# Attention's half of the output projection as 32 column-half units, half of them placed between later heads

## The chip, the cores and the metric

One core of one Trainium2 chip runs one layer of a hybrid encoder in one launch. The metric is the device time of the launch in microseconds (us); lower is better. The engines have short names in the views: PE is TensorE's matmuls, PEld its weight loads, DVE is VectorE, ACT is ScalarE, POOL is GpSimd, and SP is SyncE, which issues every transfer of this kernel. An engine works through its own queue in order; a semaphore wait stops everything behind it on that engine.

## The reference

The sequence has 2048 rows of 1024 features. After a normalisation one projection feeds two groups of heads, and one output projection takes both:

```
h    = rms_norm(x, norm_w);  proj = h @ w_in
dn   = gated_deltanet_bidir(q, k, v, beta, decay)      # 4 heads of 128, chunks, forward and backward
dn   = rms_norm(dn) * silu(z)
sw   = windowed_gqa_with_sinks(q, k, v) * silu(z)       # 8 query heads, |i-j| <= 128
out  = x + concat([dn, sw]) @ w_out                     # w_out: 1024 x 1024
```

Rows 512 to 1023 of `w_out` belong to attention (`sw`). Their product needs nothing of the delta rule, so it can be computed, added to `x` and stored as a partial result at any time between the end of attention and the last stage.

## The kernel before

Matmuls that need precision without full fp32 cost are split: an operand is copied to the fp32r type by ACT (the high part), DVE subtracts to get the low part, and three fp32r matmuls (high times high, low times high, high times low) replace one.

**phase_a** projects, convolves, runs attention (chunks of 128 rows, two groups of heads each, `attend` L327 to L378) and writes the gated attention result of each chunk to DRAM (`mix_sw`, L378).

**phase_b** has these parts, in program order:

- `pre_front(h)` (L604) loads keys, queries and values of head h, transposes them, forms the gram products `gh` (L661), multiplies them by the decay on DVE (`ma`, L670) and stores the result to DRAM (`m_d`, L675).
- `out_sw` (L564) is attention's half of the output. `load_wo` (L534) splits all of attention's rows of `w_out` (two tiles of 16 KB per partition). For each of 16 chunks it loads the mix tile once (L569), splits it (L550 on ACT, L551 on DVE), and for each of two column halves of 512 loads the rows of `x` (L555), runs 12 matmuls (L558 to L560), adds on DVE (L561) and stores a partial result (L562). Mix and split tiles have two buffers, the tag `ws` (weights in flight and `x` rows) five.
- `pre_back(h)` (L689) inverts the triangular matrices: it loads diagonal blocks (L697, L698), runs a chain of 31 pairs of dependent DVE instructions (L707, L711: the solve), stores and reloads the result (L712, L720), and assembles the inverse from 20 groups of matmuls `pi` (L735) with POOL copies between them.
- `scan(h)` (L761) is the recurrence: 16 steps, forward and backward side by side, each with five small fp32 matmuls (`pk`, `py`, `po`) joined by DVE and ACT instructions. `post` (L818) normalises and stores.
- `warm(h)` (L847) issues 32, 32 and 20 matmuls with an unused result, at the end of heads 1, 2 and 3.
- `out_dn` (L873) does the other half of the output, from the delta rule's result plus the stored partials.

`out_sw` lives in a memory pool `sw` on the right side of SBUF; the pool `hd[1]`, which holds the matrices, keys and values of heads 1 and 3, is opened after it is closed, in the same place. So nothing of head 1 can be written into `hd[1]` before the last of the 16 chunks is done.

The order on each engine isn't the program's. `set_order` (L892) lists all instructions with estimated costs, plans forwards and backwards several times with those costs, and fixes the best plan as the order of every queue. A gate in it stands for each reuse of a buffer and for each pool that takes the place of a closed one. The queue orders named below are read from the two compiled programs.

Of the kernel before, what the change touches and what calls it, by code (L numbers as in the profile page):

```python
# [7 lines left out]
F32 = mybir.dt.float32  # L8
F32R = mybir.dt.float32r
AF = mybir.ActivationFunctionType  # L10
ALU = mybir.AluOpType
# [4 lines left out]
P = 128  # L16
# [3 lines left out]
NCH = 16  # L20
# [3 lines left out]
EPS = 1e-6  # L24
NDEC = 1
NEG = -1e30


# [488 lines left out]
def phase_b(ctx, tc, t, ident, consts, hp, mix_dn, mix_sw, kq_d, v_d, zdn_d, zsw_d, dp, out):  # L517
    nc = tc.nc
    V, A, G, T = nc.vector, nc.scalar, nc.gpsimd, nc.tensor
    dma = nc.sync.dma_start  # L520

    def pool(name, bufs=1, stack=ctx, **kw):
        return stack.enter_context(tc.tile_pool(name=name, bufs=bufs, reuse_waits="tile", **kw))
# [8 lines left out]
    part_d = [dp.tile([P, D], F32, tag=f"part{c}", name=f"part{c}") for c in range(NCH)]  # L532
# [30 lines left out]

    def out_sw(pool, bank, order):  # L564
        w = load_wo(pool, 4, "s", "s")
        for n, c in enumerate(order):
            sc = slice(c * P, (c + 1) * P)
            mx = pool.tile([P, 4, P], F32, tag="mx", name=f"mxs{c}", bufs=2)
            dma(mx, mix_sw[c])  # L569
            out_half(pool, lambda j, nm: bank(n, j, nm), w, mx, t["x"][sc, :], part_d[c], f"s{c}", MB)  # L570

    MB = 2
    ORD = (7, 8, 6, 9, 5, 10, 4, 11, 3, 12, 2, 13, 1, 14, 0, 15)
    pre_stack = ctx.enter_context(ExitStack())
    with tc.using_default_side("right"):
        hd = [pool("hd0"), None]
        q1 = pool("q1")
        ps_i = [pool("ps_i0", stack=pre_stack, space=PSUM)]
        ps_t = pool("ps_t", stack=pre_stack, space=PSUM)
        ps_g = pool("ps_g", stack=pre_stack, space=PSUM)  # L580
    rp = pool("rp", 2)
    qp = pool("qp", stack=pre_stack)
    ps_s = pool("ps_s", space=PSUM)
# [20 lines left out]
    def pre_front(h):  # L604
# [12 lines left out]
        for n, c4 in enumerate(FRONT):  # L617
# [71 lines left out]
    def pre_back(h, H):  # L689
        ma = H["ma"]  # L690
        m_d, x_d, mp = H["solve"]
        L0 = qp.tile([64, 32, 32], F32, tag="L0", name=f"L0{h}")
# [7 lines left out]
        G.memset(x, 0.0)  # L700
# [146 lines left out]
    def warm(h):  # L847
        idle = ps_s.tile([P, P], F32, tag="pk", name=f"warm{h}")
        for _ in range((32, 32, 20)[h]):
            T.matmul(idle, ident, ident, start=True, stop=True)  # L850

    H = pre_front(0)
    with tc.using_default_side("right"):
        with ExitStack() as sw:
            out_sw(
                pool("sw", 5, stack=sw),
                lambda n, j, nm: ps_i[j if n >= 6 else 0].tile([P, 512], F32, tag="inv", name=nm),
                range(NCH),
            )
# [28 lines left out]

SBUF_BYTES = 229344 - 16512


def set_order(tc):  # L892
# [12 lines left out]
    def aps(l):  # L905
        return [a.bass_ap for a in l if hasattr(a, "bass_ap")]
# [142 lines left out]

# [5 lines left out]
    for k in range(total):  # L1055
        if eng[k] == "SP":
# [180 lines left out]
```

## Time and profile before

| | us |
|---|---|
| three runs | 1333.45, 1336.02, 1339.87 (median 1336.02) |
| span of the profiled execution | 1337.1 |
| PE busy | 1265.9 |
| DVE busy | 886.6 |
| ACT busy | 707.6 |
| POOL busy | 487.9 |

The launch has seven stages. Up to about 735 us it is projections, convolutions and attention. From 735 to 840 attention's last chunks run beside the front of head 0 and the first units of `out_sw`. From 840 to 896 the rest of `out_sw` runs beside the solve of head 0. Then come the four heads, bounded by the first inverse product of each: 896, 1002, 1098 and 1172 us. In each head's stage its scan runs together with the front and the solve of the next head. From 1242 us on the delta rule's half of the output runs to the end.

A matmul's busy time in these views covers its way through the array, so neighbours overlap: a busy PE isn't a PE at its peak. Where a view gives a count and a time for matmuls one after another, the time divided by the count is the better price.

### The profile page before, as it was taken

What the parts mean: (1) busy time and instruction counts of PE and PEld (TensorE: products, weight loads), DVE (VectorE), ACT (ScalarE), POOL (GpSimd) and SP (SyncE); (2) the same over time, 40 slices, a digit from 0 to 9 for tenths busy, and PEclk for the clock granted to TensorE, in tenths of its full rate; (3) what the DMA queues carried; (4) which work ended last, traced back from release to release, by engine and by line L of the source; (5) the groups of instructions that cost most, each with busy time, mean ns of one, the idle gap of its engine ahead of it and who ended that gap; (6) DMA issues with size and microseconds to landing.
All of it is one profiled execution on the core that took longest, in us unless ns stands there. A gap on an engine that the chain in (4) does not pass through costs nothing.

```text
span 1337.1 us, 22922 instructions
## 1 busy us (share of the span) xinstructions
PE 1265.9 (95%) x7330; PEld 1083.1 (81%) x7330; DVE 886.6 (66%) x2250; ACT 707.6 (53%) x2105; POOL 487.9 (36%) x876
## 2 busy tenths in 40 slices
PE   5999999999999999999999899999979989898998
PEld 4998878888789988888888678778869878798776
DVE  4413387999856324778987898567884987846433
ACT  5422254766544333334766866229757867566310
POOL 1223033575602321002677654328238247070000
PEclk8999999999999999999999999999999999999999
DMA  7442344222552444323222767968476364333776
GB/s 243 129 139 82 115 142 133 98 88 93 177 178 88 134 146 135 114 71 105 87 94 93 264 198 228 279 197 214 121 193 171 97 198 117 97 107 107 230 239 216
DMA packets 219113, 199.10 MB, mean 149 GB/s; under 512 B 48240, under 2 KB 170736, under 8 KB 218992
## 3 DMA queue, kind: packets, MB, share of 16 engines
q1 hardware_dynamic: 218992, 197.63, 48.5%
q8 instruction: 59, 0.97, 0.3%
q14 instruction: 62, 0.51, 0.1%
HBM read 132.50 MB, written 65.08 MB: 148 GB/s over the span
## 4 chain that ended last, share of the span: by engine, by line
PE 67%; DVE 10%; DMA 9%; ACT 6%; POOL 3%; issue 2%; SPq 1%; DVEq 0%; POOLq 0%; ACTq 0%
PE pf_c L186 6%; PE pf_c L187 6%; PE pf_c L188 5%; PE pf_z L186 4%; PE pf_z L187 4%; PE pf_z L188 4%; PE pi L735 3%; PE pt L360 3%; PE pq_q L197 2%; PE pq_q L198 2%; PE pq_q L199 2%; PE pcd L559 2%; PE pcd L560 2%; PE pcd L558 2%; DMA xc<-x_d 2%
## 5 line engine op out<-in xcount | busy, mean ns | idle before, releaser
L237 DVE SCALAR_TENSOR_TENSOR acc<-pf_c,cw,acc 128x512 f32<-128x512 f32 (+1 forms) x192 | 140.1, 743 | 30.4 <-ACT acc L233 27.0
L186 PE MATMUL pf_c<-xhi,wh_c 128*128 128x512 f32 x384 | 148.7, 399 | 1.7 <-DVE acc L237 1.6
L187 PE MATMUL pf_c<-xlo,wh_c 128*128 128x512 f32 x384 | 148.5, 399 | 0.0
L188 PE MATMUL pf_c<-xhi,wl_c 128*128 128x512 f32 x384 | 147.7, 397 | 0.0
L355 POOL TENSOR_SCALAR pr<-pr,st 128x384 f32<-128x384 f32 (+1 forms) x128 | 84.4, 678 | 83.5 <-DVE st L353 59.1
L188 PE MATMUL pf_z<-xhi,wl_z 128*128 128x512 f32 x256 | 94.3, 400 | 0.0
L186 PE MATMUL pf_z<-xhi,wh_z 128*128 128x512 f32 x256 | 94.1, 399 | 0.0
L187 PE MATMUL pf_z<-xlo,wh_z 128*128 128x512 f32 x256 | 93.6, 397 | 0.0
L346 ACT ACTIVATE pr<-pr,st 128x384 f32<-128x384 f32 (+1 forms) x128 | 76.0, 596 | 27.1 <-DVE st L345 24.2
L186 PEld LDWEIGHTS pf_c<-xhi,wh_c 128*128 128x128 f32 x384 | 72.1, 188 | 17.6 <-DVE acc L237 2.2
L188 PEld LDWEIGHTS pf_c<-xhi,wl_c 128*128 128x128 f32 x384 | 72.1, 188 | 15.2
L187 PEld LDWEIGHTS pf_c<-xlo,wh_c 128*128 128x128 f32 x384 | 72.1, 188 | 14.3
L364 ACT ACTIVATE ph<-pt 128x512 fp32r<-128x512 f32 x92 | 53.7, 595 | 50.1 <-PE pt L360 42.4
L341 DVE CUSTOM_DVE_ANT_0 pr<-s,mask,sink 128x384 f32<-128x384 f32 (+1 forms) x128 | 72.9, 591 | 8.4 <-PE s L340 5.7
L360 PE MATMUL pt<-ident,pr 128*128 128x128 f32 x368 | 70.8, 276 | 2.5 <-POOL pr L355 2.1
L365 DVE TENSOR_TENSOR pl<-pt,ph 128x512 fp32r<-128x512 f32 x92 | 62.0, 683 | 12.7 <-ACT ph L364 11.6
L789 ACT ACTIVATE yk<-py,ck 128x128 f32<-128x128 f32 x120 | 44.1, 367 | 43.6 <-PE py L784 40.9
L360 PEld LDWEIGHTS pt<-ident,pr 128*128 128x128 f32 x368 | 47.8, 141 | 19.0 <-POOL pr L355 5.9
L670 DVE SCALAR_TENSOR_TENSOR ma<-gh,bp,dc 128x256 f32<-128x256 f32 x128 | 56.0, 475 | 10.2 <-PE gh L661 8.1
L233 ACT ACTIVATE acc<-pf_c,cw 128x512 f32<-128x512 f32 x48 | 32.6, 682 | 54.3 <-PE pf_c L188 48.8
L197 PE MATMUL pq_q<-wh_q,xhi 128*128 128x256 f32 x256 | 58.5, 284 | 0.2 <-ACT sgq L256 0.2
L561 DVE TENSOR_TENSOR xrd<-xrd,pcd 128x512 f32<-128x512 f32 x32 | 20.9, 683 | 55.8 <-PE pcd L560 48.0
(254 smaller groups left out, 3795.2 us busy)
## 6 DMA issues: line engine op xcount, KB each, us to landing
kqc<-kq_d SPq DMA_DIRECT2D x120, 128.0 KB, 2.6
ws_c<-wt SPq DMA_DIRECT2D x48, 256.0 KB, 3.6
xr<-x SPq DMA_DIRECT2D x16, 512.0 KB, 5.7
ws_z<-wt SPq DMA_DIRECT2D x32, 256.0 KB, 3.5
kq<-kq_d SPq DMA_DIRECT2D x16, 512.0 KB, 4.9
xrs<-x SPq DMA_DIRECT2D x32, 256.0 KB, 3.9
part<-xrs SPq DMA_DIRECT2D x32, 256.0 KB, 3.4
m_d<-ma SPq DMA_DIRECT2D x32, 256.0 KB, 4.8
```

Source lines behind the costliest of these rows:

```text
L186: T.matmul(ps, hi[:, k, cs], xhi[b][:, k], start=(k == 0), stop=False)
L187: T.matmul(ps, hi[:, k, cs], xlo[b][:, k], start=False, stop=False)
L188: T.matmul(ps, lo[:, k, cs], xhi[b][:, k], start=False, stop=(k == KC - 1))
L197: T.matmul(ps[:, :n], xh, hi[:, k, :n], start=(k == 0), stop=False)
L237: V.scalar_tensor_tensor(av, ps[:, lo:], cw[:, i, k : k + 1], av, ALU.mult, ALU.add)
L341: V.tensor_tensor_reduce(pr[j][:, :n], ps[:, :n], mask[:, lo * P : hi * P], 1.0, sink[:, hh : hh + 1], ALU.add, ALU.max, accum_out=mx[:, j ...
L346: A.activation(pr[j][:, :n], pr[j][:, :n], AF.Exp, bias=nm[:, j : j + 1], accum_out=den[:, j : j + 1])
L355: G.tensor_scalar(pr[j][:, :n], pr[j][:, :n], den[:, j : j + 1], 1.0, ALU.mult, ALU.mult)
L360: T.transpose(pt[:, j], pr[j][:, (kb - lo) * P : (kb - lo + 1) * P], ident)
L364: A.activation(ph, ptf, AF.Copy)
L365: V.tensor_tensor(pl, ptf, ph.bitcast(F32), ALU.subtract)
L670: V.scalar_tensor_tensor(ma[d, c4][:, c], gh[:, k], bp[:, d, cc : cc + 1], gms[d][:, c : c + 1].to_broadcast([P, 2, P]), ALU.mult, ALU.mult,)
```

## The change

Attention's half of the output becomes 32 units, one for each chunk and column half. All 16 units of column half 0 are written between `pre_front(0)` and `pre_back(0)` in the program; of column half 1, four are written into `pre_front(2)`, four into `pre_front(3)` and eight after `pre_back(3)`; the planner is free to move them. A unit loads and splits the whole mix tile for itself, so each mix tile is loaded and split twice. Mix and split tiles have one buffer each, `ws` two; the weights are held one column half at a time.

The pool `hd1` is opened on the left, in a place of its own. Room for it comes from the smaller buffers, from a smaller reserve for software-generated transfers (`SCRATCH`, 1024 bytes), and from dropping the tile `L0`: the solve's first blocks are now loaded into `X`, copied from there into `L`, and `X` is cleared afterwards. The unused matmuls of `warm` become none. Four costs of the planner are changed. The part of the diff that matters:

```diff
+SCRATCH = 1024
+N0 = 16
+FILLF = ((0, 0, 0, 0), (1, 1, 1, 1), (1, 1, 1, 1))
+SWB = (1, 1)
+SWW = 2
...
+    def sw_units(pool):
+        w = {}
+        def weights(j):
+            wh = pool.tile([P, 4, 512], F32R, tag="wohs", name=f"wohs{j}", bufs=1)
+            wl = pool.tile([P, 4, 512], F32R, tag="wols", name=f"wols{j}", bufs=1)
...
+        def unit(c, j, bank):
+            if j not in w:
+                weights(j)
+            wh, wl = w[j]
+            ns = slice(j * 512, (j + 1) * 512)
+            mx = pool.tile([P, 4, P], F32, tag="mx", name=f"mxs{c}_{j}", bufs=SWB[0])
             dma(mx, mix_sw[c])
+            mh = pool.tile([P, 4, P], F32R, tag="mh", name=f"mhs{c}_{j}", bufs=SWB[1])
+            ml = pool.tile([P, 4, P], F32R, tag="ml", name=f"mls{c}_{j}", bufs=SWB[1])
+            A.activation(mh, mx, AF.Copy)
+            V.tensor_tensor(ml, mx, mh.bitcast(F32), ALU.subtract)
+            xr = pool.tile([P, 512], F32, tag="ws", name=f"xrs{c}_{j}")
+            dma(xr, t["x"][c * P : (c + 1) * P, ns])
...
+        todo = [(c, j) for j in range(2) for c in range(NCH)]
...
-        hd = [pool("hd0"), None]
-        q1 = pool("q1")
+        hd = [pool("hd0")]
+        q1 = pool("q1", stack=pre_stack)
+        qp = pool("qp", stack=pre_stack)
...
+    hd.append(pool("hd1"))
     rp = pool("rp", 2)
-    qp = pool("qp", stack=pre_stack)
+    swp = pool("swp", SWW, stack=pre_stack)
...
+            if h:
+                for k in range(FILLF[h - 1][n]):
+                    fill(1, bank(k % 2))
...
-        dma(L0, lv[0])
+        dma(X[0:64], lv[0])
         dma(L[64:128], lv[1])
         x = X.rearrange("p r c -> p (r c)")
+        V.tensor_copy(L[0:64], X[0:64].rearrange("p r c -> p c r"))
         G.memset(x, 0.0)
         G.memset(x[:, ::33], 1.0)
-        V.tensor_copy(L[0:64], L0.rearrange("p r c -> p c r"))
...
-        for _ in range((32, 32, 20)[h]):
+        for _ in range((0,0,0)[h]):
...
     H = pre_front(0)
-            out_sw(
...
-        hd[1] = pool("hd1")
+    for n in range(N0):
+        fill(1, bank(2 + n % 2 if n >= 6 else 2))
     pre_back(0, H)
     for h in range(3):
         scan(h, H)
         H = pre_front(h + 1)
         pre_back(h + 1, H)
         warm(h)
+    for k in range(32):
+        fill(1, bank(k % 2))
     pre_stack.close()
...
-SBUF_BYTES = 229344 - 16512
+SBUF_BYTES = 229344 - SCRATCH - 128
...
-                return max(112, m / 2.4 + 14)
+                return max(112, 0.441 * m + 4)
...
-            return 60 + 0.86 * m + 85 * (scalars > 0) + 110 * (len(o) > 1)
+            short = len(o[0].ap) > 2 and o[0].ap[-1][1] <= 64
+            return 60 + 0.86 * m + 85 * (scalars > 0) + 110 * (len(o) > 1) + 100 * short
...
-        return 150 + 1.02 * m
+        return 190 + 1.02 * m
...
+        if eng[k] == "PE" and not insts[k][0].is_transpose and "float32r" not in str(insts[k][0].ins[0].dtype):
+            lag += 40
```

More of the change, by code (lines that the diff above doesn't have):

```diff
@@ L562, in out_half, with take @@
             dma(dst[:, ns], xr)
[L564 to L568, printed above, removed]
-            dma(mx, mix_sw[c])
-            out_half(pool, lambda j, nm: bank(n, j, nm), w, mx, t["x"][sc, :], part_d[c], f"s{c}", MB)
+    def sw_units(pool):
[3 more added lines that the diff above has]
+            wl = pool.tile([P, 4, 512], F32R, tag="wols", name=f"wols{j}", bufs=1)
+            for k in range(4):
+                st = pool.tile([P, 512], F32, tag="ws", name=f"woss{j}_{k}")
+                dma(st, t["wout"][:, 4 + k, j * 512 : (j + 1) * 512])
+                A.activation(wh[:, k], st, AF.Copy)
+                V.tensor_tensor(wl[:, k], st, wh[:, k].bitcast(F32), ALU.subtract)
+            w[j] = wh, wl
+        def unit(c, j, bank):
[4 more added lines that the diff above has]
+            mx = pool.tile([P, 4, P], F32, tag="mx", name=f"mxs{c}_{j}", bufs=SWB[0])
+            dma(mx, mix_sw[c])
+            mh = pool.tile([P, 4, P], F32R, tag="mh", name=f"mhs{c}_{j}", bufs=SWB[1])
[4 more added lines that the diff above has]
+            dma(xr, t["x"][c * P : (c + 1) * P, ns])
+            ps = bank(f"pcs{c}_{j}")
+            for k in range(4):
+                T.matmul(ps, mh[:, k], wh[:, k], start=(k == 0), stop=False)
+                T.matmul(ps, ml[:, k], wh[:, k], start=False, stop=False)
+                T.matmul(ps, mh[:, k], wl[:, k], start=False, stop=(k == 3))
+            V.tensor_tensor(xr, xr, ps, ALU.add)
+            dma(part_d[c][:, ns], xr)
+        todo = [(c, j) for j in range(2) for c in range(NCH)]
+        def take(n, bank):
+            for _ in range(min(n, len(todo))):
+                unit(*todo.pop(0), bank)
+        return take
     MB = 2
@@ L691, in pre_back @@
         m_d, x_d, mp = H["solve"]
-        L0 = qp.tile([64, 32, 32], F32, tag="L0", name=f"L0{h}")
         L = qp.tile([P, 32, 32], F32, tag="L", name=f"L{h}")
@@ L848, in warm, with bank @@
         idle = ps_s.tile([P, P], F32, tag="pk", name=f"warm{h}")
-        for _ in range((32, 32, 20)[h]):
+        for _ in range((0,0,0)[h]):
             T.matmul(idle, ident, ident, start=True, stop=True)
+    fill = sw_units(swp)
+    def bank(k):
+        return lambda nm: (ps_t, ps_g, ps_i[0], ps_i[1])[k].tile([P, 512], F32, tag=("tr", "gh", "inv", "inv")[k], name=nm)
     H = pre_front(0)
-    with tc.using_default_side("right"):
-        with ExitStack() as sw:
-            out_sw(
[L856 to L859, printed above, removed]
-        hd[1] = pool("hd1")
+    for n in range(N0):
+        fill(1, bank(2 + n % 2 if n >= 6 else 2))
     pre_back(0, H)
@@ L1227 @@
     arrays = layout(inputs)
-    nc = bacc.Bacc("TRN2", target_bir_lowering=False, num_devices=1)
+    nc = bacc.Bacc("TRN2", target_bir_lowering=False, num_devices=1, dynamic_dma_scratch_size=SCRATCH)
     t = {k: nc.dram_tensor(k, v.shape, mybir.dt.from_np(v.dtype), kind="ExternalInput").ap() for k, v in arrays.items()}
```

## Prediction, made before the changed kernel ran

> **What bounds the kernel now.** I read the page first: share of time by engine, slices, chain.
>
> ```profile
> span 1337.1 us, 22922 instructions
> PE 1265.9 (95%) x7330; PEld 1083.1 (81%) x7330; DVE 886.6 (66%) x2250; ACT 707.6 (53%) x2105; POOL 487.9 (36%) x876
> ...
> PE 67%; DVE 10%; DMA 9%; ACT 6%; POOL 3%; issue 2%; SPq 1%; DVEq 0%; POOLq 0%; ACTq 0%
> ```
>
> PE carries two thirds of the chain, but its 95% is an average over unlike stages. So next comes the view of stretches, cut where the first inverse product of each head starts (columns: length; busy time and count of PE, PEld, DVE, ACT, POOL; clock; transfers).
>
> ```profile
> 50.00:735.00 685.00, 679.82 (x3667) 576.23 (x3667) 454.59 (x978) 334.62 (x745) 245.00 (x377) 1.00 0.36 114
> 735.00:840.00 105.00, 99.18 (x512) 78.32 (x511) 90.37 (x277) 78.57 (x251) 54.46 (x70) 0.98 0.72 230
> 840.00:896.00 56.00, 50.96 (x217) 40.67 (x215) 38.11 (x91) 9.01 (x21) 12.01 (x20) 0.97 0.83 259
> 896.00:1002.00 106.00, 91.39 (x652) 81.75 (x652) 81.67 (x263) 78.44 (x350) 51.80 (x111) 0.98 0.65 169
> 1002.00:1098.00 96.00, 86.80 (x647) 79.82 (x648) 72.66 (x239) 72.18 (x302) 48.62 (x97) 0.97 0.59 162
> 1098.00:1172.00 74.00, 67.83 (x517) 62.42 (x518) 56.00 (x189) 44.82 (x167) 33.96 (x90) 0.98 0.39 106
> 1172.00:1242.00 70.00, 64.39 (x514) 60.52 (x512) 38.87 (x122) 48.46 (x176) 26.44 (x77) 1.00 0.39 116
> 1242.00:1337.00 95.00, 90.26 (x396) 72.23 (x395) 33.87 (x59) 15.79 (x42) 1.64 (x1) 0.99 0.67 225
> ```
>
> Up to 735 us and from 1242 us PE is the bound, and the work there is unchanged. ACT falls from 78.57 of 105 us to 9.01 of 56 at 840 us: attention is over. What then fills 840 to 896? The same view for attention's output units alone, then the chain in order of time:
>
> ```profile
> 735.00:840.00 105.00, 49.89 (x176) 31.73 (x177) 9.51 (x14) 0.98 0.72 230
> 840.00:896.00 56.00, 50.09 (x209) 39.68 (x207) 12.32 (x18) 0.97 0.83 259
> ```
>
> ```profile
> 840.59 6.57 DMA m_d<-ma
> 847.22 5.68 DMA L<-m_d
> ...
> 887.98 2.73 DMA x_d<-X
> 891.14 2.75 DMA xc<-x_d
> ...
> 896.20 1.17 PE pi L735 x8
> ...
> 1258.30 0.91 PE pcd L560 x4
> ```
>
> Two things share this stage: 209 unit matmuls (17 units of 12), and head 0's solve, from the store of `ma` at 840.59 to its result at 887.98. Four 512-wide matmuls take 0.91 us, so a unit is 12 x 0.2275 = 2.73 us and 17 take 47 of 56 us. Both end at about 890: removing units alone gains nothing unless the solve comes earlier too.
>
> In the heads PE works at less than its peak, and in the stretches with a solve DVE is nearly full:
>
> ```profile
> 1040.00:1080.00 40.00, 35.51 (x263) 31.41 (x262) 38.05 (x131) 31.02 (x136) 8.68 (x10) 1.00 0.39 113
> 1120.00:1160.00 40.00, 35.91 (x280) 33.00 (x279) 36.58 (x131) 24.41 (x93) 12.20 (x24) 1.00 0.28 80
> ```
>
> **The change part by part.** In the changed PE queue 16 units stand ahead of head 0's inverse, 9 of them behind attention, with head 1's front among them; 3 in scan 0, 4 in scan 1, 2 in the gap after it, 4 in scan 2, 1 in the gap after that, 2 in scan 3. So 16 units, 16 x 2.73 = 44 us of PE, leave the stage before 896 and must fit into the 346 us of the heads. The prices:
>
> ```profile
> L670 DVE SCALAR_TENSOR_TENSOR ma<-gh,bp,dc 128x256 f32<-128x256 f32 x128 | 56.0, 475 | 10.2 <-PE gh L661 8.1 <-ACT dc L669 1.4
> L850 PE MATMUL warm<-ident 128*128 128x128 f32 x168 | 23.6, 284 | 0.0
> L561 DVE TENSOR_TENSOR xrs<-xrs,pcs 128x512 f32<-128x512 f32 x32 | 21.8, 682 | 19.6 <-PE pcs L560 15.5 <-DMA xrs<-x 3.5 <-DMA xc<-x_d 0.4
> L551 DVE TENSOR_TENSOR mls<-mxs,mhs 128x512 fp32r<-128x512 f32 x16 | 11.0, 689 | 0.0
> L543 DVE TENSOR_TENSOR wols<-woss,wohs 128x512 fp32r<-128x512 f32 x8 | 5.8, 738 | 2.4 <-ACT wohs L542 2.3
> ```
>
> *Front (before 896).* DVE's work up to the end of solve 0 hardly changes. Out go about 15 additions (15 x 0.68 = 10.2 us) and four weight splits (4 x 0.74 = 3.0). In come 24 products `ma` of head 1 (24 x 0.475 = 11.4) with about 4 us of small operations: +2. But head 0's products now stand ahead of the last attention chunk, so the solve need not wait through the 18 idle DVE us of 840 to 896 (56 - 38.1). I count on 10 of these 18: -10 + 2 = **-8**. Bounds: -16, if all are won; +8, below, if the buffers pace the units. Behind the copy that opens the solve stands the rest of attention on DVE, so a late load of `L` would stall that too.
>
> *Scan 0's stage (106 us).* Head 1's front (32 `ma`) is done before it, as `hd1` no longer waits for the units. That takes 32 x 0.475 = 15 us off DVE's 81.67; three units and the last weight splits add 3 x (0.68 + 0.69) + 3 x 0.74 = 6: 73 us. At this stage's own filling (81.67 of 106, 0.77) 73 us of work take 95; at the fullest stretch's (38.05 of 40, 0.95) 77. I take 92, near the first, as solve 1 can now start with the scan and no longer in its middle: **-14**. Bounds: -29 and 0. What is late next is the scan itself: its 16 steps bound the stage, not the solve.
>
> *Scan 1's and 2's stages (96 and 74 us).* Each gets 4 to 6 units beside a full DVE: 4 x 1.37 = 5.5 us. The solve also gets a wait: POOL may clear `X` only after DVE has copied from it, and DVE's first solve operation waits for POOL.
>
> ```profile
> L700 POOL MEMSET X<- x4: 951/954/959, 843.9 to 1089.1; 128x1024 f32 x4
> ```
>
> That is 0.95 us, with a small second clear and two hand-overs an estimated 1.5 us, for heads 2 and 3, where the solve is late. Behind the waiting solve operation stand the scan's own DVE steps, for which PE and ACT wait; behind the clear on POOL the running head's inverse copies. I take **+4** and **+6**: less for stage 1, whose first half has DVE idle (72.66 busy of 96). Bounds: 0 and +16 each (6 units x 2.73, nothing hidden).
>
> *Scan 3's stage.* Two units beside a DVE busy 38.87 of 70: **+1**; bounds -2 and +5.
>
> *Unused matmuls removed.*
>
> ```profile
> 1172.88 1.50 PE L850 MATMUL warm<-ident 128*128 128x128 f32 x12
> ```
>
> ```profile
> 1000.00:1010.00 10.00, 7.72 (x43) 7.72 (x44) 3.56 (x11) 5.43 (x26) 9.33 (x20) 0.66 0.82 210
> ```
>
> (A line of the order in time, then a stretch.) Twelve records take 1.50 us, the last alone 0.28, so one is (1.50 - 0.28) / 11 = 0.11 and all 168 are 18.7 us of PE. They fill waits of the inverse; I take **-2**, bounds -6 and +10 (the clock, below).
>
> *SP's queue:* in the heads it gets 16 mix loads, 16 loads of `x` and 16 stores among the scan's loads; a store that waits for its addition holds back the loads behind it. The scan's loads run up to four steps ahead (four buffers), which hides a wait of some us; if that cover is gone, it is part of (b).
>
> *At no cost:* 16 more loads and ACT splits of mix tiles (ACT at most 78.4 of 106 busy, transfers 0.39 to 0.65 in the heads); the smaller scratch, as this row holds all but 1.48 of 199.10 MB:
>
> ```profile
> q1 hardware_dynamic: 218992, 197.63, 48.5%
> ```
>
> New planner costs reorder neighbours before 735 us too; PE idles only 5.2 of 685 us there, so +-4.
>
> **Sum:** -8 - 14 + 4 + 6 + 1 - 2 = -13. Span 1337.1 - 13 = 1324; the span lies 1.1 above the median of 1336.0, so **1323 us**.
>
> **Rivals.** (a) *The units ride free.* PE idles 346 - 310.4 = 35.6 us in the heads and the removed matmuls free 18.7 more, above the 44 needed. Then front -16, scan 0 -14, nothing given back: -30, **1306**. Against it: the full DVE above.
>
> (b) *The units pay in full (slower).* Both queues are in order: a unit that waits for its mix tile holds up the scan's next matmul. The 13 units after scan 0 cost 13 x 2.73 = 35.5; with -8, and -14 + 8 for scan 0: +21.5, less some of the 18.7 removed, say 7: +14, **1350**. It decides when the stages of scans 1 to 3 together grow by over 22 us (240 to 262).
>
> (c) *One buffer paces the units.*
>
> ```profile
> xrs<-x SPq DMA_DIRECT2D x32, 256.0 KB, 3.9
> part<-xrs SPq DMA_DIRECT2D x32, 256.0 KB, 3.4
> ...
> mxs<-mix_sw SPq DMA_DIRECT2D x16, 256.0 KB, 4.3
> ```
>
> ```profile
> L550 ACT ACTIVATE mhs<-mxs 128x512 fp32r<-128x512 f32 x16 | 10.1, 632 | 40.8 <-PE pcs L560 34.3 <-DVE X L711 6.4
> ```
>
> The next mix load starts when DVE has split the last: 4.3 + 0.63 (ACT) + 0.69 = 5.6 us a unit, 50 us for nine behind attention's end (840 in the rows; about 833 with DVE relieved of the 13 us above), to 883: just beside the solve. Two `ws` buffers give (3.9 + 2.7 + 0.7 + 3.4) / 2 = 5.4 us for the rows of `x`, about the same. If mix load, split and matmuls don't overlap, a unit is 5.6 + 2.7 = 8.3 and nine end at 908, 12 late; as idle PE takes on head 1's front meanwhile, I price the front at +8 in place of -8: **1339**, no change. The Trainium skill (Trainium Kernel Development and Optimization, Best Practices) says "Double-buffer for performance: Overlap DMA with compute", which speaks for (c); no run here shows the single buffer yet.
>
> (d) *The clock falls.* Even with the unused matmuls the granted clock was 0.66 in 1000 to 1010 (row above): 0.34 x 10 = 3.4 us of PE. Without them each of three gaps between scans may lose as much: +10, **1333**. The Trainium skill (TensorE: Matmul & The Clock Gate, Part 1: The HAM clock gate) has the array at half clock after an idle window of about 3.4 us; the trace agrees as far as a 0.66 average over 10 us goes.
>
> That the change doesn't do what it says is excluded for order: the queues show the units moved.
>
> **How the numbers follow.** Forecast 0.42, its own range 1314 to 1334; (a) 0.20; (b) 0.18; (c) 0.10; (d) 0.05; 0.05 for reordering before 735. The range for 8 in 10 reaches from (a) down by 4 to nearly (b): 1302 to 1348. A measurement tells about 0.5% (6.7 us) from no change. Faster by more: 0.36 of the forecast, 0.20 of (a), 0.01 of the rest, 0.57. Slower: (b) 0.18, 0.02 of (c), 0.04 of the rest, 0.24. Within: 0.19.
>
> **What would show it.** First inverse product at about 888 (was 896.20); its successors 92, 100, 80 and 71 us apart. If (a), the stages of scans 1 to 3 stay at 240 together. If (b), they pass 262. If (c), the first inverse product is at 896 or later with PE idle before it, waiting for splits of mix tiles. If (d), the clock of the gaps falls under 0.66. Wrong altogether would be a shift of over 5 us before 735.

## The result and the profile after

The changed kernel takes 1332.8 us (median of 19 runs, 1326.86 to 1338.15) where the kernel before took 1336.0 beside it: ratio 0.9961, 95% interval 0.9948 to 0.9973, about 5 us less. The forecast was 13 us less. Its profiled execution has a span of 1333.9 us (1337.1 before); at 1335.6 us it is one of the slower of the 19. The page:

```profile
span 1333.9 us, 22667 instructions
PE 1251.8 (94%) x7162; PEld 1061.5 (80%) x7162; DVE 894.0 (67%) x2266; ACT 719.9 (54%) x2121; POOL 494.8 (37%) x876
...
PE 65%; DVE 14%; DMA 6%; ACT 6%; POOL 4%; issue 4%; SPq 0%; DVEq 0%; ACTq 0%; POOLq 0%
...
L597 PE MATMUL pcs<-wohs,mhs 128*128 128x512 f32 x128 | 58.4, 457 | 17.4 <-ACT mhs L591 9.2
...
mxs<-mix_sw SPq DMA_DIRECT2D x32, 256.0 KB, 3.8
```

PE is busy 14 us less, with 168 records less, yet the span is 3 us less: idle time took most of it. The units' first matmuls wait 17.4 us in all, more than half of it for ACT's split of the mix tile. Before the change they waited 3.5:

```profile
L558 PE MATMUL pcs<-wohs,mhs 128*128 128x512 f32 x128 | 52.3, 411 | 3.5 <-DVE xrs L561 2.5 <-ACT mhs L550 0.3 <-ACT wohs L542 0.3
```

The same view of stretches as for before, cut at the first inverse product of each head (columns: length; busy time and count of PE, PEld, DVE, ACT, POOL; clock; transfers):

```profile
745.00:840.00 95.00, 82.96 (x416) 60.96 (x417) 82.58 (x259) 73.73 (x244) 57.71 (x77) 0.96 0.71 212
840.00:906.00 66.00, 49.76 (x203) 35.53 (x201) 46.85 (x129) 33.56 (x141) 16.88 (x24) 0.92 0.80 243
906.00:985.00 79.00, 72.19 (x546) 66.31 (x547) 65.09 (x210) 56.01 (x211) 42.27 (x93) 1.00 0.61 165
985.00:1085.00 100.00, 90.94 (x653) 81.57 (x652) 81.20 (x264) 80.44 (x337) 49.79 (x98) 1.00 0.74 209
1085.00:1170.00 85.00, 79.75 (x566) 72.01 (x567) 63.35 (x205) 50.93 (x184) 36.23 (x90) 0.96 0.57 159
1170.00:1239.00 69.00, 66.23 (x505) 61.36 (x503) 39.63 (x124) 43.99 (x153) 26.27 (x79) 1.00 0.39 117
```

The stage before the first product has PE idle for 16 of 66 us, where before it was 5 of 56, and the clock there fell from 0.97 to 0.92. Set beside the forecast's terms (the products start at 906.0, 985.3, 1085.5 and 1170.5 us, the last stage at 1238.6):

| | before | after | change | forecast |
|---|---|---|---|---|
| first product of head 0 at | 896.2 | 906.0 | +9.8 | -8 |
| to that of head 1 | 106.1 | 79.3 | -26.8 | -14 |
| to that of head 2 | 95.6 | 100.2 | +4.6 | +4 |
| to that of head 3 | 74.1 | 85.0 | +10.9 | +6 |
| to the last stage | 69.4 | 68.2 | -1.2 | +1 |

What sets 906.0 is read in the chain of the changed kernel in order of time:

```profile
898.97 1.14 ACT jk L690 x8
900.11 0.94 ACT dc L710 x4
901.15 0.37 ACT vs L723
901.53 0.53 ACT mhs L591
902.08 0.69 DVE mls L592
902.77 0.23 DVE xt L764
...
903.05 0.29 POOL iv L771
...
905.98 0.29 POOL iv L771
```

`xt` transposes head 0's reloaded blocks for the inverse. Its first block had landed at 899.7 us, but on DVE it stands behind the low part of the sixteenth unit, and that waits for the high part on ACT. The unit's mix tile had landed at 898.6; ACT was still busy with the keys, decays and values of head 1 (`jk`, `dc`, `vs`), so `xt` came 3 us late. SP's own order in time leads to the other part:

```profile
889.07 0.67 SPq L755 DMA_DIRECT2D x_d<-X  x1
...
892.31 0.33 SPq L664 DMA_DIRECT2D vt<-v_d  x1
893.05 0.33 SPq L601 DMA_DIRECT2D part<-xrs  x1
894.73 0.32 SPq L588 DMA_DIRECT2D mxs<-mix_sw  x1
895.10 0.43 SPq L716 DMA_DIRECT2D m_d<-ma  x1
895.62 0.47 SPq L763 DMA_DIRECT2D xc<-x_d  x1
897.53 0.53 SPq L662 DMA_DIRECT2D kq<-kq_d  x1
898.83 0.36 SPq L716 DMA_DIRECT2D m_d<-ma  x1
899.25 0.50 SPq L763 DMA_DIRECT2D xc<-x_d  x1
...
902.37 0.42 SPq L763 DMA_DIRECT2D xc<-x_d  x1
...
904.85 0.99 SPq L763 DMA_DIRECT2D xc<-x_d  x1
```

and before:

```profile
887.98 0.33 SPq L712 DMA_DIRECT2D x_d<-X  x1
889.17 0.32 SPq L562 DMA_DIRECT2D part<-xrs  x1
890.72 0.92 SPq L720 DMA_DIRECT2D xc<-x_d  x2
...
893.86 0.43 SPq L720 DMA_DIRECT2D xc<-x_d  x1
...
895.00 0.42 SPq L720 DMA_DIRECT2D xc<-x_d  x1
```

The solve's result leaves at nearly the same time, 889.07 and 887.98. Its store lands 6.4 us after its issue instead of 2.7. At its issue six transfers of head 1's front and of the units stand ahead of it on SP's queue that haven't landed yet, and before the change one. The first reload is issued as soon as the store has landed, in both kernels, and lands 4.1 us later instead of 2.1. The view of these two transfers (`x_d`, store and first reload), first after the change, then before:

```profile
DMA to landing us min/median/max: 4.1/5.3/6.4
```

```profile
DMA to landing us min/median/max: 2.1/2.4/2.7
```

So the first block is there 10.7 us after the store's issue instead of 4.8. The second reload is issued 3.6 us after the first instead of 0.4, because transfers of head 1's front (`kq`, `m_d`), which wait for its products, now stand between them; the third and fourth land after the first product has started. (The mix load waits until 894.7 for the one buffer, but the store lands only at 895.5, so that wait is not what holds the first reload.) From the store to the first product it takes 16.9 us instead of 8.2: some 9 us are lost behind a solve that ended at nearly the same time.

### The profile page after: what moved, and what is told of

Its sections match the earlier page's. It is cut to its first block, busy times and chain, and to the rows that moved or that the text cites. A ratio compares the mean times of both kernels' runs of the same rounds, so it can differ in the third digit from the quotient of the medians.

```text
span 1333.9 us, 22667 instructions
## 1 busy us (share of the span) xinstructions
PE 1251.8 (94%) x7162; PEld 1061.5 (80%) x7162; DVE 894.0 (67%) x2266; ACT 719.9 (54%) x2121; POOL 494.8 (37%) x876
## 4 chain that ended last, share of the span: by engine, by line
PE 65%; DVE 14%; DMA 6%; ACT 6%; POOL 4%; issue 4%; SPq 0%; DVEq 0%; ACTq 0%; POOLq 0%
PE pf_c L191 5%; PE pf_c L193 5%; PE pf_c L192 5%; PE pi L778 4%; PE pf_z L192 4%; PE pf_z L193 4%; PE pf_z L191 4%; DVE acc L242 3%; PE pq_q L202 2%; PE pcd L564 2%; PE pcd L565 2%; PE pt L365 2%; PE pcd L563 2%; PE pq_q L203 2%; PE pq_q L204 2%
## 5 line engine op out<-in xcount | busy, mean ns | idle before, releaser
L242 DVE SCALAR_TENSOR_TENSOR acc<-pf_c,cw,acc 128x512 f32<-128x512 f32 (+2 forms) x192 | 140.7, 745 | 26.2 <-ACT acc L238 24.1
L193 PE MATMUL pf_z<-xhi,wl_z 128*128 128x512 f32 x256 | 90.4, 400 | 0.0
L191 PE MATMUL pf_z<-xhi,wh_z 128*128 128x512 f32 x256 | 89.7, 400 | 0.0
L192 PE MATMUL pf_z<-xlo,wh_z 128*128 128x512 f32 x256 | 89.1, 399 | 0.0
L597 PE MATMUL pcs<-wohs,mhs 128*128 128x512 f32 x128 | 58.4, 457 | 17.4 <-ACT mhs L591 9.2
L183 DVE TENSOR_TENSOR wl_c<-ws_c,wh_c 128x512 fp32r<-128x512 f32 x48 | 35.9, 752 | 36.8 <-ACT wh_c L182 24.1
```

Of the source, the lines that this page charges most:

```text
L191: T.matmul(ps, hi[:, k, cs], xhi[b][:, k], start=(k == 0), stop=False)
L192: T.matmul(ps, hi[:, k, cs], xlo[b][:, k], start=False, stop=False)
L193: T.matmul(ps, lo[:, k, cs], xhi[b][:, k], start=False, stop=(k == KC - 1))
L242: V.scalar_tensor_tensor(av, ps[:, lo:], cw[:, i, k : k + 1], av, ALU.mult, ALU.add)
L597: T.matmul(ps, mh[:, k], wh[:, k], start=(k == 0), stop=False)
```

## The experiments

Each kernel ran beside the kernel before on the same chip; ratios are to it. The tables give the start of head 0's first inverse product and the time from unit to unit (start of the eighth to start of the sixteenth, over eight).

### Two buffers and fewer units ahead

`mix2`, `split2`, `both2` and `n8`:

```diff
 # mix2; split2 has (1, 2); both2 has (2, 2) and oacc 5 -> 4
-SWB = (1, 1)
+SWB = (2, 1)
-... name=f"jk{h}_{c4}_{j}_{c}", bufs=3)   # the same for jko
+... name=f"jk{h}_{c4}_{j}_{c}", bufs=2)
-... name=f"kqc{nm}", bufs=4)
+... name=f"kqc{nm}", bufs=3)
 # n8: this edit alone
-N0 = 16
+N0 = 8
```

> The mix tile of a unit gets two buffers, the split still one; to make room, kqc goes from 4 buffers to 3 and jk and jko from 3 to 2. Buffer theory: in the changed kernel a unit between 840 and 905 us takes 6 to 8 us because the next mix piece is issued only when VectorE has read the last one (0.33 us issue, 4.4 us to landing, 0.63 us ScalarE, 0.69 us VectorE, and the waits between them); with two buffers the piece is there, a unit takes 4 to 5 us, the sixteenth unit starts before 885 us instead of at 902, and head 0's first inverse product moves from 906.0 us to about 897 (the solve ends near 888). Total 1324 if the 9 us are kept. Solve theory (the solve itself, slowed by head 1's product tiles on VectorE, is what the product waits for): product stays at 903 to 907, total 1331 to 1335. Give-back theory: product moves to 897, and the scans behind it take it back; total 1331 to 1335.

> The split pair of a unit gets two buffers, the mix tile one; the same three reductions as in the run with two mix buffers, so that this run is also the check on these. Buffer theory, if the mix piece paces the units: nothing moves by over 2 us, first inverse product of head 0 at 904 to 907 us, total 1331 to 1335. If instead the release of the split by the last matmul paces them (2.7 us of matmuls ahead of the next 0.63 us on ScalarE): unit falls to 5 us here, product at 897, total about 1325.

> Two buffers for the mix tile and for the split, with the reductions of the other two and oacc from 5 buffers to 4. Buffer theory: the units are no longer a chain; 3 to 4 us each, the sixteenth starts before 878 us; the product is then set by the solve and moves to 893 to 897 us. Total 1322 to 1325. Solve theory: product at 903 to 907, total 1331 to 1335. Give-back theory: product at 893 to 897, total 1331 to 1335, with head 1's to head 3's stages longer by the same 9 us.

> Only eight units stand ahead of head 0's first inverse product (all of them beside attention), the other 24 between later heads and the last scan. Buffer theory: PE's queue is clear once the solve ends; product at about 893 to 897 us instead of 906, but eight more units of 2.73 us of matmuls (22 us) go into the stages behind it, where PE idles 7 us between 906 and 985, 9 us between 985 and 1085, 5 us between 1085 and 1170 and 3 us between 1170 and 1239; so 9 to 11 us won ahead and up to 22 us less the cover paid behind: total 1330 to 1345. Solve theory: product at 903 to 907 us and total 1340 to 1357.

| | ratio, 95% | product | unit |
|---|---|---|---|
| changed kernel | 0.9961 (0.9948 to 0.9973) | 906.0 | 7.2 |
| mix2 | 0.9886 (0.9857 to 0.9915) | 887.6 | 5.4 |
| split2 | 0.9957 (0.9935 to 0.9979) | 899.7 | 7.5 |
| both2 | 0.9990 (0.9973 to 1.0006) | 909.7 | 5.2 |
| n8 | 0.9970 (0.9954 to 0.9986) | 876.0 | - |

The mix buffer paces the units, the split's doesn't. The units alone in each window, in the changed kernel and in mix2 (columns: length; busy time and count of PE, PEld, DVE; clock; transfers):

```profile
844.00:902.00 58.00, 31.45 (x96) 20.07 (x96) 5.47 (x8) 0.91 0.83 255
```

```profile
831.00:874.00 43.00, 27.59 (x97) 17.07 (x95) 4.71 (x7) 1.00 0.88 268
```

Eight units (96 matmuls) take 58 us with one mix buffer and 43 with two, and the clock stays at 1.00. DVE is busy for 41.2 of the 44.6 us of head 0's solve in mix2 and for 43.5 of 55.1 in the changed kernel, so the solve's result leaves at 868.3 instead of 889.1. The stretch behind it gains nothing: from the store to the first product it takes 19.3 us here, 16.9 in the changed kernel, so the single buffer isn't what lengthens it. both2 is a miss: its first weight load is issued at 794 us instead of mix2's 747 (why wasn't tried; its pool is 4 KB larger and may lie on tiles that are freed later), and the product came at 909.7. n8 moved the product 30 us ahead, and its total is that of the changed kernel: the stages behind it became 29 us longer for eight units more. That looked like a clear case for the buffer. It wasn't one yet.

### Parts put back on top of two mix buffers

```diff
 # m_n32
-N0 = 16
+N0 = 32
 # m_mlpool: low part of the later units on GpSimd
-            V.tensor_tensor(ml, mx, mh.bitcast(F32), ALU.subtract)
+            (V if len(todo) >= 32 - N0 else G).tensor_tensor(ml, mx, mh.bitcast(F32), ALU.subtract)
 # m_warm
-        for _ in range((0,0,0)[h]):
+        for _ in range((32, 32, 20)[h]):
 # m_oldcost: the four planner costs of the kernel before
```

> The version with two mix buffers, with all 32 units ahead of head 0's first inverse product and none between the later heads. Place theory (the stage from head 0's first inverse product to head 1's fell from 106 to 79 us because head 1's tiles no longer wait for the units' space): head 1's first solve step still starts at 905 to 920 us, some 20 us or more ahead of the last unit, where before it came 57 us after the last unit (891 to 948). Fewer-units theory (it fell because 16 units less stand in PE's queue ahead): the units end near 930, and head 1's first solve step comes 50 us later, at 975 to 990. VectorE theory (the later stages grew by 5 and 11 us because each unit takes 1.4 us of a VectorE that is busy 88% there): the stages from head 1's to head 2's and from head 2's to head 3's first inverse product fall from 99.9 and 83.5 to about 95 and 75. Otherwise they stay. Total by place and VectorE theories 1315 to 1330, by fewer units 1340 to 1360.

> The version with two mix buffers; the 16 units of the later heads make the low part of the split on GpSimd instead of VectorE. VectorE theory: five or six units in each of the stages behind head 1 and head 2 give 3.4 to 4.1 us of VectorE back in each; both stages fall by 3 to 5 us, total 6 to 10 us below the version with two mix buffers. If VectorE's sum does not set these stages but the order of the solve's steps does: no change within 3 us, or 2 to 6 us longer where the subtraction (an estimate from the same operation's 0.68 us on VectorE: 1.0 to 1.5 us) stands ahead of the inverse's assembly on GpSimd.

> The version with two mix buffers, with the 84 unused matmuls of the kernel before put back behind the heads' scans. Prediction's term: 2 us longer. If they fill only idle time of TensorE: no change within 1.5 us. If they keep the granted clock up in the later stages: 1 to 4 us shorter, with fewer half-clock pieces behind 890 us.

> The version with two mix buffers, with the planner's old costs for the float32r matmul, the short ScalarE rows, GpSimd and the lag of matmuls. Prediction: worth nothing by themselves, so within 3 us of the version with two mix buffers. If the order that the new costs give is what made the stage behind head 0 shorter: that stage back from 82 towards 106 us, total 10 to 25 us longer.

| | ratio, 95% | product | unit |
|---|---|---|---|
| m_n32 | 1.0247 (1.0223 to 1.0271) | 969.5 | 6.9 |
| m_mlpool | 0.9969 (0.9958 to 0.9981) | 897.4 | 5.8 |
| m_warm | 0.9964 (0.9950 to 0.9979) | 891.9 | 5.6 |
| m_oldcost | 0.9981 (0.9965 to 0.9997) | 886.1 | 5.7 |

m_n32 bears out the place of `hd1`, though its total was missed by over 40 us: the 32 units end at 969 instead of near 930, and the granted clock from 850 to 970 us was 0.87. The first line is head 1's solve before the change, the second in m_n32; the third and fourth are the last kind of unit matmul in the same two kernels (after the count come the shortest, median and longest in ns, then the first and last start).

```profile
L707 DVE TENSOR_TENSOR tm<-L,X x31: 173/359/1181, 948.3 to 985.3; 128x31 f32<-128x31 f32 x2, 128x60 f32<-128x60 f32 x2, 128x87 f32<-128x87 f32 x2, 128x112 f32<-128x112 f32 x2
```

```profile
L750 DVE TENSOR_TENSOR tm<-L,X x31: 192/374/426, 928.2 to 960.2; 128x31 f32<-128x31 f32 x2, 128x60 f32<-128x60 f32 x2, 128x87 f32<-128x87 f32 x2, 128x112 f32<-128x112 f32 x2
```

```profile
L560 PE MATMUL pcs<-wols,mhs x128: 387/389/628, 756.2 to 893.5; 128*128 128x512 f32 x128
```

```profile
L599 PE MATMUL pcs<-wols,mhs x56: 388/389/402, 911.8 to 969.3; 128*128 128x512 f32 x56
```

Before, head 1's solve starts 55 us after the last unit matmul, 893.5 to 948.3. In m_n32, with all 32 units ahead, it starts 41 us before the last, 928.2 against 969.3. The later stages, without units, took 108.3 and 69.9 us, not 95 and 75: together 5 us less than mix2, where 13 were expected.

The other three all lost 10 to 13 us against mix2, a subtraction on another engine as much as 84 matmuls. Their units and first products (886 to 897) stayed ahead of the changed kernel's. So either mix2 stands on a peak, or something other than the edits moved.

### Other orders of equal programs, and two parts on the kernel before

The planner writes a new order of all five queues for any edit. mix2_kqc4 keeps four kqc buffers; mix2_lag changes one planner figure; b_nowarm and b_newcost are the kernel before with one part of the change.

```diff
 # mix2_lag
-            lag += 40
+            lag += 30
 # b_nowarm
-        for _ in range((32, 32, 20)[h]):
+        for _ in range((0, 0, 0)[h]):
```

> The version with two mix buffers, but kqc keeps its 4 buffers (only jk and jko go from 3 to 2). Each edit lets the planner write another order of the whole program, so this is a second order with the same two mix buffers. Buffer theory (two mix buffers are worth what the first version showed): total within 5 us of that version, 1318 to 1328 where the kernel before has 1338. Order theory (the planner's orders of equal programs lie about 10 us apart, and the first version is a good one): total anywhere in 1322 to 1337, and head 0's first inverse product still at 885 to 900 us.

> The version with two mix buffers, with one planner figure changed by a quarter: the lag behind a full-precision matmul from 40 to 30 ns. The program computes and loads the same; only the order moves. Buffer theory: within 5 us of the version with two mix buffers, 1318 to 1328. Order theory: anywhere in 1322 to 1337, with head 0's first inverse product at 885 to 900 us; then differences under some 10 us between single variants say nothing of the edit that made them.

> The kernel before with its 84 unused matmuls (168 passes) taken out, nothing else. Prediction's term: 2 us shorter, since they fill TensorE's idle time. Ledger theory (putting them back cost the version with two mix buffers 10 us, and TensorE's busy time grows by 11 us with them): 8 to 12 us shorter, 1326 to 1330. Clock theory: without them the granted clock falls more often behind 990 us, and the time grows by 1 to 5 us.

> The kernel before with the planner's new costs alone. Prediction: within 3 us of before. Cost theory (going back to the old costs took 13 us from the version with two mix buffers): 8 to 14 us shorter, about 1327. Order theory: within 10 us of before on either side, for the order alone.

| | ratio, 95% | product | unit |
|---|---|---|---|
| mix2_kqc4 | 0.9993 (0.9975 to 1.0010) | 900.5 | 5.7 |
| mix2_lag | 0.9924 (0.9897 to 0.9950) | 891.3 | 5.4 |
| b_nowarm | 0.9973 (0.9953 to 0.9992) | 906.6 | - |
| b_newcost | 1.0027 (1.0008 to 1.0046) | 904.8 | - |

The order theory holds. Three orders with two mix buffers lie between 0.9886 and 0.9993, 14 us apart, with nearly the same unit time. Totals of single variants can't price an edit here below some 10 us, and those of the table above don't. Stage times and waits can. So the 3.6 us that b_nowarm is shorter (1 to 6 by the interval) lie near the forecast's 2 but don't price the unused matmuls either. (By the pages TensorE's busy time is 15.2 us lower in b_nowarm than before and 21.6 higher in m_warm than in mix2, not the 11 of the expectation.) The first product moves with the order as well: two more orders of the kernel before have it at 906.6 and 904.8, where the kernel before has 896.2.

### The order held

Now the planner is told the old buffers or the old sizes, so that every queue has the changed kernel's order, instruction for instruction. fix_two has two mix buffers in that order (and jk and jko with two, to make room), fix_add leaves out most of VectorE's sum in the later units. a_lag and ctl are two more orders with single buffers.

```diff
 # fix_two
-SWB = (1, 1)
+SWB = (2, 1)
+TOLD = {("swp", "mx"): 1, ("q1", "jk"): 3, ("rp", "jko"): 3}
...
-            home[f"{tag}_{name}_{p.id}"] = (name, m.bufs)
+            bufs = TOLD.get((name, tag), m.bufs)
...
+            home[f"{tag}_{name}_{p.id}"] = (name, bufs)
 # fix_add, with the planner's cost left at 512 columns
-            V.tensor_tensor(xr, xr, ps, ALU.add)
+            e = 512 if len(todo) >= 32 - N0 else 16
+            V.tensor_tensor(xr[:, :e], xr[:, :e], ps[:, :e], ALU.add)
```

> The changed kernel, instruction for instruction in its own order on all five queues (the planner is told one mix buffer and three jk and jko), but with two mix buffers in the chip (jk and jko have two to make room). So the buffer alone, without a new order. Buffer theory: eight units from the eighth to the sixteenth at 5.2 to 5.7 us each instead of 7.2, as in the three versions with two mix buffers; head 0's first inverse product at 889 to 897 us instead of 906; total 6 to 12 us under the changed kernel, at 0.987 to 0.992 of before. Order theory: the orders made for two buffers were what was better; here unit spacing and product stay within 3 us of the changed kernel, total at 0.995 to 0.998 of before.

> The changed kernel in its own order on all five queues; in the 16 units of the later heads, VectorE's sum of residual and product is made for 16 of 512 columns only (so half of the attention part of the output lacks its product), 0.68 us down to some 0.1 us each. VectorE theory (the later stages grew because VectorE, busy 88% there, has the units' work too): 16 times 0.6 us, 9 us, of which 6 to 9 show in the total, 0.988 to 0.992 of before, and the stage from head 2's to head 3's first inverse product at 80 to 83 us instead of 85. TensorE theory (a unit costs its 2.7 us of matmuls there, VectorE's part lies beside): under 2 us, 0.994 to 0.998.

> The changed kernel with the one planner figure changed as before (lag behind a full-precision matmul 30 for 40 ns): another order of the same program with single buffers. Order theory: total anywhere in 0.989 to 1.003 of before, as the three orders with two mix buffers spread over 0.989 to 0.999; the eighth to sixteenth units stay at 7 us or more each and the product of head 0 at 900 to 910. If the order hardly matters: 0.994 to 0.998.

> The changed kernel with only the three reductions (kqc 3, jk 2, jko 2) that the first versions with two buffers had: the control for them, and one more order with single buffers. If the reductions themselves cost or gain nothing: within the spread of orders, 0.989 to 1.003, units at 7 us or more, product at 900 to 910 us. If the smaller kqc were what helped the first version with two mix buffers: about 0.988.

| | ratio, 95% | product | unit |
|---|---|---|---|
| fix_two | 0.9945 (0.9929 to 0.9962) | 901.1 | 7.2 |
| fix_add | 0.9947 (0.9927 to 0.9967) | 900.1 | 7.0 |
| a_lag | 0.9957 (0.9945 to 0.9970) | 907.0 | 7.5 |
| ctl | 0.9926 (0.9906 to 0.9946) | 900.2 | 7.1 |

The units alone in fix_two, columns as above:

```profile
840.00:897.00 57.00, 31.33 (x96) 19.88 (x94) 5.47 (x8) 0.91 0.82 251
```

My buffer theory falls in its plain form: the second buffer alone changes nothing, 57 us for eight units against 58. In the order made for one buffer, SP issues the next mix load where that order had it, behind transfers that wait for other things: on average 0.6 us ahead of the end of the last low part, against 0.2 us after it in the changed kernel. In mix2 it is 5.4 us ahead, and a unit takes 5.4 us. It takes the buffer and an order that uses it. (The reverse, mix2's order with one buffer, wasn't tried: its SP queue has the next load ahead of what frees the one buffer.)

VectorE's sums of the later units cost nothing that shows either: from 0.68 us down to 0.17 each the ratio is 0.9947, and the stage to head 3's product 86.6 us instead of 85.0.

### The later units' matmuls taken out

```diff
 # fix_mm: fix_add, and its matmuls as narrow, order held
-                T.matmul(ps, mh[:, k], wh[:, k], start=(k == 0), stop=False)
+                T.matmul(ps[:, :e], mh[:, k], wh[:, k, :e], start=(k == 0), stop=False)
...
 # m_n12: mix2 with
-N0 = 16
+N0 = 12
```

> The changed kernel in its own order on all five queues; the 16 units of the later heads multiply and add for 16 of 512 columns only (the right half of the output lacks attention's product in the other columns). Their twelve matmuls each go from about 2.7 us to an estimate of under 0.8 us, from the 64 ns a pass that the unused 128-column passes added to TensorE's busy time. TensorE theory (behind head 0 a unit costs about its matmuls, since nothing covers them): 16 times 2 us, 32 us, of which 20 to 32 show from head 0's first inverse product to the last output stage, 300 to 313 us where the changed kernel has 333, and the stage from head 2's to head 3's product at 73 to 78 us instead of 85; total 1300 to 1315. Cover theory (the forecast's: the units lie in TensorE's idle time there and cost little): that stretch at 325 us or more, total over 1325.

> Two mix buffers with twelve units ahead of head 0's first inverse product instead of sixteen; the other 20 between and behind the later heads. Buffer theory: four units at 5.4 us less ahead of the product, so it moves from 888 towards 870 us, as far as the solve lets it. TensorE theory: four units more behind it, at about 2 to 3.7 us each, 8 to 15 us back. Together 0 to 10 us either way of the version with sixteen, 1315 to 1332, within the spread of the planner's orders.

fix_mm: ratio 0.9951 (0.9933 to 0.9970), no less than fix_add's. From the first product to the last stage 334.0 us (changed kernel 332.6). m_n12: 0.9987 (0.9972 to 1.0001), product 895.5 (its solve ended at 868), within the spread of orders. Both theories for fix_mm are answered by its stretches from the first product on, columns as for the changed kernel:

```profile
895.00:974.00 79.00, 69.47 (x549) 64.92 (x549) 64.86 (x210) 55.73 (x212) 42.76 (x94) 1.00 0.60 168
974.00:1074.00 100.00, 87.71 (x653) 80.52 (x652) 77.92 (x264) 80.44 (x337) 50.28 (x100) 0.96 0.74 212
1074.00:1159.00 85.00, 76.88 (x567) 72.86 (x566) 60.34 (x206) 50.92 (x185) 35.32 (x88) 0.90 0.56 156
1159.00:1229.00 70.00, 64.85 (x497) 61.55 (x498) 37.37 (x121) 43.32 (x153) 26.42 (x80) 0.95 0.38 113
```

PE is busy 298.9 of 334 us, in the changed kernel 309.1 of 333: idle 35 against 24. The clock takes 0.04 x 100 + 0.10 x 85 + 0.05 x 70 = 16 us, in the changed kernel 0.04 x 85 = 3.4. So by an estimate from these figures, which charges the lower clock to busy time alone, some 23 us of matmuls at full speed went (309.1 - 3.4 against 298.9 - 16; 32 were expected). 11 came back as idle time and 13 as a lower clock, in stages of nearly the same 79, 100 and 85 us. As far as the idle time goes, the units lie in time that PE has to wait through anyway, as the cover theory has it. What the other half would have given at an unchanged clock isn't shown. At the clock that was granted, the length of these stages did not follow PE's work.

The best version is mix2: 0.9886 of the kernel before, 0.9857 to 0.9915, 1322.4 us, ahead of both kernels. It is the changed kernel with a second mix buffer in one good order; its neighbours show that the order has its share.

## Why the prediction was wrong in size

**The direction was right, the size wasn't:** about -5 against -13. In the profiled execution the front and head 0's stage together gave -17.0 where -22 was forecast, the two stages behind them +15.5 where +10 was. The direction rests on a second miss: head 0's stage won 13 us more than forecast, and the front lost 18 more. By the forecast's own steps:

1. *Front, -8: the step that failed.* It counted on winning 10 of the 18 idle DVE us ahead of the solve's end, and let the rest of the way to the first product stand as it was. The times cut at the end of the last projection (`pf_z`) and at the store of the solve's result (`x_d`), with the three other executions of the same order:

| us | projections end at | to the solve's store | to the first product |
|---|---|---|---|
| before | 731.3 | 156.7 | 8.2 |
| changed kernel | 740.2 | 148.8 | 16.9 |
| fix_two | 738.4 | 146.0 | 16.6 |
| fix_add | 737.3 | 146.8 | 15.9 |
| fix_mm | 734.5 | 144.9 | 15.9 |
| mix2 | 736.3 | 132.0 | 19.3 |

   The part that was priced came in, in size: the way to the store is 7.9 us shorter, in the other three 10 to 12. That is partly luck, as it is the balance of two larger moves: the solve starts at 833 instead of 853 and, beside head 1's products, takes 55 us instead of 35. What the forecast had at nothing took it back. The way from the store to the first product grew by some 8 us in all four executions (7.7 to 8.7), through the later landings and the queues read above; in two more orders of the kernel before, b_nowarm and b_newcost, it is 9.1 and 8.6. The forecast priced SP's queue only for the scans. And the projections end 3 to 9 us later. The forecast gave +-4 for this and called a shift of over 5 us before 735 "wrong altogether"; three of the four executions are over it. With the planner's new costs alone (b_newcost) they end at 732.3; what delays them stays open. The four first products lie at 906.0, 901.1, 900.1 and 895.4, a mean of 900.6, +4.4 and so 12 from the forecast.

   Rival (c), with 0.10, had its sign come true: the product after 896, and PE idle before it, waiting for splits. Its 8.3 us a unit and "nine end at 908" stand against 7.2 and 905.6, its +8 against +9.8. But the late units are only a part of the way to the product, the 3 us that `xt` stands behind the last low part. That the units' pace needs the buffer and the order together is shown by fix_two against mix2; how much of the total it costs is not, as the orders with one buffer (0.9926 to 0.9961) and with two (0.9886 to 0.9993) overlap. The Trainium skill's rule that the forecast set beside (c), to double-buffer for overlap (Trainium Kernel Development and Optimization, Best Practices), holds only with the order: 58 us for eight units with one buffer, 57 with two in the same order, 43 with two in an order of their own.

2. *Head 0's stage, -14 (bounds -29 and 0): right mechanism, too small.* It measured -26.8. m_n32 shows the cause: head 1's solve no longer waits for the last unit. b_nowarm shows a share of another term: without the unused matmuls alone, head 1's product came at 996.5 instead of 1002.3. So of the 17 us that the changed kernel is ahead there (985.3), 6 may be theirs or the new order's, in one execution each.

3. *Stages of scans 1 and 2, +4 and +6: right in sign, +4.6 and +10.9 in size, the cause not borne out.* The forecast charged VectorE's part of the units, 1.37 us each. fix_add took 0.5 of that away and fix_mm the matmuls too, and the stages stayed at 101.0 and 86.6, then 100.1 and 85.3. The other part of it, the subtraction, wasn't tried in this order. The length goes with the order: a_lag, another order of the same program, has 101.2 and 80.1, ctl 96.5 and 81.4, in one execution each (the same order has 85.0 to 88.5 for the second). The wait for POOL's clear of `X` was priced in the same terms and not tried by itself; its share stays open.

4. *Unused matmuls, -2:* -3.6 on the kernel before, in one other order. (Their 18.7 us of PE are 18.6 by the forecast's own division.) Rival (d) gave as its sign a clock under 0.66 in the gaps between scans, and it didn't come: in the changed kernel the heads have a clock of 1.00 in three of the four stages, and one fall of 6.8 us before 1170, as long as the one behind 1001 before. Its mean over the runs is 0.990; the clock's falls moved from the heads to the front (0.92). b_nowarm has a mean of 0.984 over its runs where the kernel before has 0.992, but b_newcost, with all its unused matmuls, has 0.986, so an order alone can do that. The Trainium skill (TensorE: Matmul & The Clock Gate, Part 1: The HAM clock gate) has the fall after an idle window of some 3.4 us. Here PE was idle, by its records, for 2.2, 2.0 and 1.7 of the 3.4 us before the three falls between 840 and 906, and for 0.7 before the one at 835, so less than a whole window without a matmul on record is enough.

5. *Planner's costs, +-4:* b_newcost +3.6 us, in one order. The forecast had no term for the order itself, which in these runs is worth 5 us among single-buffer versions and 14 among those with two. That is as large as the whole forecast.

6. *Rivals (a) and (b)* set the test at 240 us and at 262 for the stages of scans 1 to 3 together. They took 253.4 (239.1 before), between the two. (b)'s price of a unit, its 2.73 us of matmuls, isn't borne out at the clock that was granted: in fix_mm, by the estimate above, 23 us of them went and the stages stayed. (a) is borne out in part: about half of these 23 us had lain in time that PE waits through, but the stages grew all the same.

## What to carry to other kernels

A second buffer is worth something only if the queue that issues the load reaches it early: look at what stands ahead of the load in the issuing engine's order. A transfer that the next stage waits for can land late behind transfers that were moved ahead of it, so price the way from a result to its first use anew. Where a planner reorders the program on each edit, run an order of the same program beside the edit, or hold the order, before a few us are put down to the edit. And matmuls that go from a stage with waits are not time won: look first whether the wait, or the clock, takes their place.

## What the runs showed of the hardware that was not expected

The granted clock answered to work that was taken out of stages that wait. fix_mm, with 192 matmuls at 16 of 512 columns, has a mean clock of 0.982 over its runs, fix_add in the same order 0.991. In its profile fix_mm stayed at half clock for up to 13.7 us at a time (from 1152 us), where the changed kernel's longest fall was 6.8.

The same store of 512 KB (`x_d`) landed 2.7 us after its issue in the kernel before, 6.4 in the changed kernel and 6.7 in mix2. One, six and seven transfers that hadn't landed yet stood ahead of it on SP's queue. In b_nowarm, with none, it took 2.8.

Executions of one program differ by the clock as well: over the changed kernel's 19 runs a mean clock lower by 0.01 goes with about 6 us more (correlation -0.67).
